# A decoder layer on one core: the order of the work between a residual product and the next product, rewritten

## The chip, the cores and the metric

The kernel runs on one core of a Trainium2 chip. The metric is the device time of one execution in microseconds. The kernel before took 2469.97 us, the median of three runs between 2469.17 and 2472.55.

## The reference

A decoder layer on 256 tokens of 2048 numbers, all in float32. Three sublayers follow, each in the same frame: normalise, modulate by two rows of a conditioning vector, compute, multiply by a gate row, add to x.

```python
mod = (c_act @ w_ada[l] + b_ada[l]).reshape(b, N_MOD, D_MODEL)     # 9 rows of 2048
h = modulate(rms_norm(x, norm_ffn1[l]), mod[:, 0], mod[:, 1])
x = x + 0.5 * mod[:, 2][:, None, :] * swiglu(h, w_ffn1_gu[l], w_ffn1_down[l])
h = modulate(rms_norm(x, norm_mix[l]), mod[:, 3], mod[:, 4])
x = x + mod[:, 5][:, None, :] * token_mixing(h, w_in[l], w_ret_branch[l], w_swa_branch[l],
                                              w_out[l], sinks[l])
h = modulate(rms_norm(x, norm_ffn2[l]), mod[:, 6], mod[:, 7])
x = x + 0.5 * mod[:, 8][:, None, :] * swiglu(h, w_ffn2_gu[l], w_ffn2_down[l])
return rms_norm(x, norm_final)
```

`swiglu` is a product to 2x5632 columns, a gating, and a product back to 2048 (5632 deep). `token_mixing` begins with one wide product `h @ w_in`, from which retention, sliding-window attention and two branch gates take their columns, and ends with the product by `w_out`. The attention's keys are the columns at `O_SK` and its values those at `O_SV`.

## The kernel before

**Tiles.** Tokens are held in two halves t of 128, the depth in blocks kb of 512 (four rows of 128), the columns in chunks of 512. The weights are streamed once. SP's queue loads a block of 512x512 weights as a `raw` tile of 1 MB (`load`, from a pool of four), in the written order.

**Split products.** Every operand of a product is split in two, a rounded part (a cast on ACT) and a remainder (a subtraction on DVE), and each product is the sum of three matmuls: rounded by rounded (L322), remainder of the activation by rounded weight (L323), rounded activation by remainder of the weight (L324). A half block of weights, 128x1024, is cast at L330 (`wh`) and its remainder taken at L331 (`wl`); the pool behind them holds three of each. Splits that have to live longer go to a `home` tile (L402, L403), one of four `slot` buffers. The activations of a residual product are split at L362 and L363 (`a`, or `home`), those of a product behind a normalisation are kept in `Held`, rounded `hh` and remainder `hl`. A half block times both halves of the tokens is 12 matmuls, times one half 6, a whole block times both halves 24.

**The residual product** (`down_product`) stands three times in the program: behind the first SwiGLU, behind the token mixing (by `w_out`), behind the second SwiGLU. It does chunks 0 and 1 first. Of chunks 2 and 3 (`banks[0]` and `banks[1]`) the last three depth blocks, a-1, a and b, are ordered by hand: a loop in which chunk 2 is multiplied, while the weights of chunk 3 are split ahead and kept (`late`), then chunk 3 for t=0 (`last(0, steps)`), then six steps (`tail`) of chunk 3 for t=1, handed to the passage that follows. `add_gated` multiplies a bank by the gate row (L512), adds it to `x_sb` (L513) and has ACT square the result and sum it along the row (L431). `ssq` collects the sums.

**The passage** (`into_norm`, its `before` and `after`) stands behind the first two residual products and runs into the first chunk of the next product (`head`): the `O_SK` chunk of `w_in` the first time, the first gate chunk of the second SwiGLU the second time. `inv_rms` makes the reciprocal root from the sums (L443 to L457). Then the normalised half goes through in four blocks of 512 columns: `normed` scales a block (L477, `x0` to `x3`), `turned` transposes it on PE (L484), `hold` modulates it in four slices, the first ones on ACT (L496), the others on DVE (L498), casts it (L504) and takes the remainder (L505). Two banks hold transposed blocks. A third user of `down_product` is the final normalisation (`final`), which multiplies by the gain row (L1128), scales (L1140, L1144) and sends each chunk out (L1145) through four buffers.

**What sets the order.** A scheduler places the instructions of PE, DVE, ACT and POOL by its own estimate of time; DMAs on SP's queue stay in written order. Within `tc.manual_schedule(engines=ORDERED)` PE, DVE and ACT keep the written order among the instructions of that block, but what is written behind the block may still be placed among them. Such work is the conditioning: `conditioning` loads `w_ada` in rows (L198) and multiplies and sums them on DVE (L203), a step at a time, paced by `set_pace` and `tick` over the half blocks of the products that follow.

**Around the first passage**, POOL's queue copies `x_sb` to memory (`x_d`, L825), since `skt`, the transposed keys, takes the same buffer, loads a few constants (L811, L817, L818) and clears `skt` (L829, L830) and `sv`, the values (L833).

## Time and profile before

| | |
|---|---|
| runs | 2469.17 to 2472.55 us, median 2469.97 of 3 |
| span of the profiled execution | 2465.2 us |
| median less span | 4.8 us, which lie around the span |
| busy: PE | 2410.9 us, 98% of the span, 10910 instructions |
| busy: PE's weight loads | 1981.8 us, 80% |
| busy: DVE | 1701.6 us, 69% |
| busy: ACT | 1195.0 us, 48% |
| busy: POOL | 13.4 us |

The times in the profile are microseconds from the start of the span, of one execution. A line of the timeline gives start, duration, engine, source line, operation, what it writes and from what, and in brackets how long the engine idled before it and for whom. PE's matmuls are pipelined, so the duration of one is longer than the distance between two. The first passage with its residual product's last part lies between 746.79 and 814.20, the second between 1683.11 and 1745.50, the third residual product's last part ends at 2454.45.

### The profile page before, as it was taken

How to read it: one execution, taken by the hardware profiler on the slowest of the kernel's cores; microseconds unless marked ns; L12 is line 12 of the kernel's file. 1: busy time of each engine (PE TensorE's matmuls, PEld its weight loads, DVE VectorE, ACT ScalarE, POOL GpSimd, SP SyncE). 2: the span in 40 equal slices, each digit the busy share in tenths (PEclk: the TensorE clock that was granted, in tenths of full speed). 3: DMA queues.
4: the chain of work that ended last, by engine and by line, in shares of the span. 5: the costliest groups of instructions: out<-in, count | busy, mean ns of one | idle time of the engine just before them, and what ended most of it. 6: DMA issues, size and time to landing. Idle time of an engine off the chain costs nothing. (4 is left out here: it accounts for less than half of the span.)

```text
span 2465.2 us, 29158 instructions
## 1 busy us (share of the span) xinstructions
PE 2410.9 (98%) x10910; PEld 1981.8 (80%) x10910; DVE 1701.6 (69%) x2728; ACT 1195.0 (48%) x1623; POOL 13.4 (1%) x21
## 2 busy tenths in 40 slices
PE   7999999999998999999999999999999999999998
PEld 4778888888786888888888888887788888888886
DVE  6898877777876676786666776767655555545656
ACT  6544544444545554554544444455544444444544
POOL 0000000000000000000000000000000000000000
PEclk9999999999999999999999999999999999999999
DMA  9987687888875665557677777755566666665563
GB/s 355 339 335 268 235 312 297 326 304 303 313 254 206 236 224 205 188 191 253 223 257 255 256 256 257 281 188 179 203 236 227 222 228 232 222 222 191 188 201 120
DMA packets 244656, 603.27 MB, mean 245 GB/s; under 512 B 9697, under 2 KB 10081, under 8 KB 225185
## 3 DMA queue, kind: packets, MB, share of 16 engines
q1 hardware_dynamic: 243010, 591.61, 67.1%
q0 software_dynamic: 1504, 9.81, 1.1%
q8 instruction: 85, 1.39, 0.2%
q14 instruction: 57, 0.47, 0.1%
HBM read 597.16 MB, written 4.22 MB: 244 GB/s over the span
## 5 line engine op out<-in xcount | busy, mean ns | idle before, releaser
L331 DVE TENSOR_TENSOR wl<-raw,wh 128x1024 fp32r<-128x1024 f32 (+1 forms) x828 | 996.6, 1209 | 602.8 <-ACT wh L330 601.3
L330 ACT CAST wh<-raw 128x1024 fp32r<-128x1024 f32 (+1 forms) x828 | 862.6, 1043 | 1044.5 <-PE pa L323 1016.4
L322 PE MATMUL pa<-wh,hh 128*128 128x512 f32 x2224 | 871.9, 393 | 3.8 <-ACT wh L330 2.9
L323 PE MATMUL pa<-wh,hl 128*128 128x512 f32 x2224 | 872.3, 392 | 1.8 <-DVE hl L472 1.8
L324 PE MATMUL pa<-wl,hh 128*128 128x512 f32 x2224 | 805.3, 393 | 3.0 <-DVE wl L331 2.9
L322 PEld LDWEIGHTS pa<-wh,hh 128*128 128x128 f32 x2224 | 418.1, 188 | 93.6 <-ACT wh L330 4.8
L324 PEld LDWEIGHTS pa<-wl,hh 128*128 128x128 f32 x2224 | 416.0, 188 | 92.0 <-DVE wl L331 7.9
L323 PEld LDWEIGHTS pa<-wh,hl 128*128 128x128 f32 x2224 | 418.5, 188 | 87.9 <-DVE hl L472 2.5
L323 PE MATMUL pa<-wh,a 128*128 128x512 f32 x992 | 383.9, 389 | 0.0
L324 PE MATMUL pa<-wl,a 128*128 128x512 f32 x992 | 367.5, 390 | 1.3 <-DVE wl L331 1.2
L322 PE MATMUL pa<-wh,a 128*128 128x512 f32 x992 | 367.2, 390 | 0.3 <-DVE t L512 0.2
L324 PEld LDWEIGHTS pa<-wl,a 128*128 128x128 f32 x992 | 185.7, 188 | 42.2 <-DVE wl L331 4.0
L322 PEld LDWEIGHTS pa<-wh,a 128*128 128x128 f32 x992 | 186.1, 188 | 40.5 <-DVE t L512 0.9
L323 PEld LDWEIGHTS pa<-wh,a 128*128 128x128 f32 x992 | 186.1, 188 | 38.5
L203 DVE CUSTOM_DVE_ANT_0 slot<-slot,cact 128x512 f32<-128x512 f32 (+1 forms) x252 | 193.0, 816 | 27.6 <-DMA slot<-in_w_ada_dram 27.4
L203 DVE CUSTOM_DVE_ANT_0 raw<-raw,cact 128x512 f32<-128x512 f32 (+1 forms) x260 | 167.0, 697 | 36.2 <-DMA raw<-in_w_ada_dram 25.8
L363 DVE TENSOR_TENSOR a<-slot,a 128x512 fp32r<-128x512 f32 x124 | 85.0, 686 | 12.3 <-ACT a L362 12.3
L362 ACT CAST a<-slot 128x512 fp32r<-128x512 f32 x124 | 76.1, 615 | 14.7 <-PE pa L324 14.7
L413 ACT COPY slot<-ps 128x512 f32<-128x512 f32 x75 | 41.7, 586 | 26.3 <-PE ps L412 25.9
L203 DVE DVE_READ_ACCUMULATOR2_ANT sums<- 128x1 f32 x512 | 43.3, 85 | 0.0
L431 ACT ACTIVATE pd<-x_sb 128x512 f32<-128x512 f32 x32 | 19.1, 596 | 42.1 <-DVE x_sb L513 39.4
L412 PE MATMUL ps<-small_c,t 128*128 128x128 f32 x272 | 37.7, 272 | 0.0
(170 smaller groups left out, 1061.6 us busy)
## 6 DMA issues: line engine op xcount, KB each, us to landing
raw<-in_w_ffn_gu_dram SPq DMA_DIRECT2D x152, 1024.0 KB, 5.0
raw<-in_w_in_dram SPq DMA_DIRECT2D x104, 1024.0 KB, 5.0
raw<-in_w_ffn_down_dram SPq DMA_DIRECT2D x88, 1024.0 KB, 5.1
slot<-in_w_ada_dram SPq DMA_DIRECT2D x76, 1024.0 KB, 7.6
raw<-in_w_ada_dram SPq DMA_DIRECT2D x64, 1024.0 KB, 4.8
raw<-in_w_ffn_gu_dram SPq DMA_DIRECT2D x24, 768.0 KB, 6.4
raw<-in_w_swa_branch_dram SPq DMA_DIRECT2D x16, 1024.0 KB, 5.2
raw<-in_w_ret_branch_dram SPq DMA_DIRECT2D x16, 1024.0 KB, 5.3
```

The source lines that it names most:

```text
L203: nc.vector.tensor_tensor_reduce(out=w[:, at], in0=w[:, at], in1=cact[:, at], scale=1.0, scalar=0.0, op0=ALU.mult, op1=ALU.add, accum_out= ...
L322: nc.tensor.matmul(ps, ah[:, j, ts], wh[:, j, :], start=first, stop=False)
L323: nc.tensor.matmul(ps, al[:, j, ts], wh[:, j, :], start=False, stop=False)
L324: nc.tensor.matmul(ps, ah[:, j, ts], wl[:, j, :], start=False, stop=last)
L330: nc.scalar.copy(hi, src)
L331: nc.vector.tensor_sub(lo, src, hi.bitcast(F32))
L362: nc.scalar.copy(hi, v)
L363: nc.vector.tensor_sub(lo, v, hi.bitcast(F32))
L412: nc.tensor.transpose(ps[:, j * P : (j + 1) * P], src_of(j), ident)
L413: nc.any.tensor_copy(dest, ps[:, : n * P])
L431: nc.scalar.activation(side_bank(), src, AF.Square, accum_out=dest)
```

## The change

In `down_product` the loop over the last three blocks splits late weights only in its step a (block a of chunk 3). Those of a-1 and of b are split behind the loop. The products of chunk 3 begin with three half blocks in the order t=0, t=1, t=0, so that `tail` holds five steps of t=1 instead of six. The addition of chunk 2 for t=0 stands ahead of `before`, in which the next product's first weights are split, and the one for t=1 behind it.

In the passage, `hold` becomes `Block`, whose `modulate` (slices and cast) and `rest` (remainder) are called apart, and a half block of weights becomes a `Piece`, whose `cast` and `rest` are called apart. Both halves of weight block 1 are cast ahead of the addition of chunk 3 for t=0. Three blocks of t=0 are scaled before the first transposition, the fourth much later. Weight blocks 2 and 3 are split in pieces between the blocks, partly into `home` tiles. At the end the first weight block of the chunk after the head (`c1`) is split too and handed on as `ready`, and a fence for the scheduler, `tc.no_sync_barrier()`, closes the passage: it keeps what is written behind it from being placed ahead of it, and makes no engine wait.

The conditioning begins eight half blocks later (`idle`). The product of the `O_SV` chunk is written ahead of the transpositions of the keys, and `skt` and `sv` are cleared by DVE behind these, no longer by POOL.

```diff
...
-    def set_pace(outputs, halves, place, ahead):
+    def set_pace(outputs, halves, place, ahead, idle=0):
...
         pace["steps"] = conditioning(outputs, place, ahead)
-        pace["rate"] = len(outputs) * KD * AQ / halves
-        pace["due"] = 0.0
+        pace["rate"] = len(outputs) * KD * AQ / (halves - idle)
+        pace["due"] = -idle * pace["rate"]
...
+    class Piece:
+        def __init__(self, raw, h, home=None, at=0):
+            self.src = raw[:, 2 * h : 2 * h + 2, :]
+            if home is None:
+                self.hi = wsp.tile([P, 2, CH], F32R, tag="wh", name=nm("wh"))
+                self.lo = wsp.tile([P, 2, CH], F32R, tag="wl", name=nm("wl"))
...
+        def cast(self):
+            nc.scalar.copy(self.hi, self.src)
+        def rest(self):
+            nc.vector.tensor_sub(self.lo, self.src, self.hi.bitcast(F32))
...
+    class Block:
...
+            self.h4, self.hi, self.lo = h4, self.held.hi[:, at[0], at[1]], self.held.lo[:, at[0], at[1]]
+            nc.scalar.copy(self.hi, h4)
+            return self
+        def rest(self):
+            nc.vector.tensor_sub(self.lo, self.h4, self.hi.bitcast(F32))
...
             a, b = nb - 2, nb - 1
             home = home_tile().rearrange("p i (h n) -> p (i h) n", h=2)
             pairs, late = {}, {}
+            def late_product(t, kb, h):
+                piece = late[kb, h]
+                products(
+                    banks[1], *pairs[kb][h], piece.hi, piece.lo,
+                    kb + h == 0, kb == b and h == 1, [t],
+                )
+            def late_pieces(kb):
+                raw, place = load(w, kb, c0s[1]), home_tile()
+                for h in range(2):
+                    late[kb, h] = Piece(raw, h, place, h).both()
             for kb in (a - 1, a, b):
-                wt = weight(w, kb, c0s[0])
+                raw = load(w, kb, c0s[0])
                 pairs[kb] = []
                 for h in range(2):
+                    piece = Piece(raw, h).both()
                     place = None
                     if kb >= a:
                         place = home[:, (kb - a) * 2 + h].rearrange("p (i n) -> p i n", i=2)
                     pairs[kb].append(act.pair(kb * 2 + h, place))
                     products(
-                        banks[0], *pairs[kb][h], *wt(h), kb + h == 0, kb == b and h == 1
+                        banks[0], *pairs[kb][h], piece.hi, piece.lo,
+                        kb + h == 0, kb == b and h == 1,
                     )
-                n = kb + 1 if kb < b else a - 1
-                wt = weight(w, n, c0s[1], None if n < a else home_tile())
-                late[n] = [(n, h, wt(h)) for h in range(2)]
-            steps = [step for kb in (a - 1, a, b) for step in late[kb]]
-            def last(t, which):
-                for kb, h, (wh, wl) in which:
-                    products(
-                        banks[1], *pairs[kb][h], wh, wl, kb + h == 0, kb == b and h == 1, [t]
-                    )
-            last(0, steps)
+                if kb == a:
+                    late_pieces(a)
+            raw = load(w, a - 1, c0s[1])
+            for h in range(2):
+                late[a - 1, h] = Piece(raw, h).both()
+            late_product(0, a - 1, 0)
+            late_product(1, a - 1, 0)
+            late_product(0, a - 1, 1)
+            late_pieces(b)
+            for kb in (a, b):
+                for h in range(2):
+                    late_product(0, kb, h)
+            add_gated(banks[0][0], 0, c0s[0], gate, ssq)
+            root_table()
             before()
-            root_table()
-            for t in range(NT):
-                add_gated(banks[0][t], t, c0s[0], gate, ssq)
+            add_gated(banks[0][1], 1, c0s[0], gate, ssq)
             after(
                 ssq,
                 lambda t: add_gated(banks[1][t], t, c0s[1], gate, ssq),
-                [lambda i=i: last(1, steps[i : i + 1]) for i in range(6)],
-            )
-    def into_norm(m_shift, w, c0):
+                [
+                    lambda kb=kb, h=h: late_product(1, kb, h)
+                    for kb, h in ((a - 1, 1), (a, 0), (a, 1), (b, 0), (b, 1))
+                ],
+            )
+    def into_norm(m_shift, w, c0, c1):
         held = Held()
-        nb = KD // KB
         banks = []
-        parts = {}
+        parts, ready = {}, []
         def before():
-            wt = weight(w, 0, c0, home_tile())
+            raw, place = load(w, 0, c0), home_tile()
             for h in range(2):
-                parts[0, h] = wt(h)
+                parts[0, h] = Piece(raw, h, place, h).both()
         def after(ssq, add, tail):
+            def half(t, kb, h):
+                k2 = kb * 2 + h
+                products(
+                    banks, *held.pair(k2), parts[kb, h].hi, parts[kb, h].lo,
+                    k2 == 0, 2 * k2 + 2 == KD, [t],
+                )
             def head(t, kb):
                 for h in range(2):
+                    half(t, kb, h)
+            def block(t, kb, ps, on_act):
+                return Block(held, t, kb, ps, m_shift).modulate(on_act)
+            raw = load(w, 1, c0)
+            for h in range(2):
+                parts[1, h] = Piece(raw, h)
+            parts[1, 0].both()
+            parts[1, 1].cast()
             add(0)
+            parts[1, 1].rest()
+            tail[0]()
+            tail[1]()
             r0 = inv_rms(ssq, 0)
+            raw = load(w, 2, c0)
+            parts[2, 0] = Piece(raw, 0)
+            parts[2, 0].cast()
             x0 = normed(0, r0, 0)
             x1 = normed(0, r0, 1)
             tail[2]()
             tail[3]()
             p0 = turned(x0)
+            x2 = normed(0, r0, 2)
+            b00 = block(0, 0, p0, 2)
+            p1 = turned(x1)
             tail[4]()
+            b01 = block(0, 1, p1, 3)
+            b00.rest()
+            p2 = turned(x2)
+            add(1)
+            b01.rest()
+            banks.extend(acc_bank() for _ in range(NT))
+            head(0, 0)
+            r1 = inv_rms(ssq, 1)
+            b02 = block(0, 2, p2, 4)
+            x0 = normed(1, r1, 0)
+            parts[2, 0].rest()
+            b02.rest()
+            x1 = normed(1, r1, 1)
+            half(0, 1, 0)
+            p0 = turned(x0)
+            half(0, 1, 1)
+            both = home_tile()
+            parts[2, 1] = Piece(raw, 1, both, 0)
+            raw = load(w, 3, c0)
+            parts[3, 0] = Piece(raw, 0, both, 1)
+            parts[2, 1].cast()
+            b10 = block(1, 0, p0, 2)
+            x3 = normed(0, r0, 3)
+            parts[2, 1].rest()
+            b10.rest()
+            parts[3, 0].cast()
+            half(0, 2, 0)
             p1 = turned(x1)
+            half(0, 2, 1)
+            b11 = block(1, 1, p1, 3)
+            parts[3, 0].rest()
+            b11.rest()
+            half(1, 0, 0)
+            p3 = turned(x3)
+            half(1, 0, 1)
+            x2 = normed(1, r1, 2)
+            b03 = block(0, 3, p3, 3)
+            b03.rest()
             p2 = turned(x2)
+            head(1, 1)
+            x3 = normed(1, r1, 3)
+            b12 = block(1, 2, p2, 3)
+            parts[3, 1] = Piece(raw, 1, home_tile(), 0)
+            parts[3, 1].cast()
+            b12.rest()
+            parts[3, 1].rest()
             p3 = turned(x3)
+            head(1, 2)
+            block(1, 3, p3, 3).rest()
+            head(0, 3)
+            head(1, 3)
+            raw = load(w, 0, c1)
+            ready.extend(Piece(raw, h).both() for h in range(2))
+            tc.no_sync_barrier()
+        return held, banks, ready, before, after
...
-    held, head, *calls = into_norm(3, wi, O_SK)
+    held, head, ready, *calls = into_norm(3, wi, O_SK, O_SV)
...
-    set_pace([(7, 2, None), (6, None, None), (5, None, 1.0)], 262, raw_row, 2)
+    set_pace([(7, 2, None), (6, None, None), (5, None, 1.0)], 262, raw_row, 2, 8)
...
-    nc.gpsimd.memset(skt[HD:, 0], 0.0)
-    nc.gpsimd.memset(skt[:HD, 1], 0.0)
     VW = HD + KVH * P
-    sv = slot()[:, : NT * VW].rearrange("p (t n) -> p t n", t=NT)
-    nc.gpsimd.memset(sv, 0.0)
-    b = head
+    b = in_chunk(O_SV, ready)
...
-    b = in_chunk(O_SV)
+    nc.vector.memset(skt[HD:, 0], 0.0)
+    nc.vector.memset(skt[:HD, 1], 0.0)
+    sv = slot()[:, : NT * VW].rearrange("p (t n) -> p t n", t=NT)
+    nc.vector.memset(sv, 0.0)
...
-    held, head, *calls = into_norm(6, w_ffn2_gu[0], 0)
+    held, head, ready, *calls = into_norm(6, w_ffn2_gu[0], 0, DFF)
...
-    set_pace([(8, None, 0.5)], 160, raw_row, 2)
-    ffn_up(held, w_ffn2_gu[0], tiles, 0, head)
+    set_pace([(8, None, 0.5)], 160, raw_row, 2, 8)
+    ffn_up(held, w_ffn2_gu[0], tiles, 0, head, ready)
...
```

With `home` a `Piece` takes its place there. `gemm`, `gemm_part` and `ffn_up` pass `ready` through and use it in place of a first load and split. The old lines of the passage's `after`, which stand in the listing above, are left out of the diff; its lines that carry no sign were there, in another place or the same.

Of the changed kernel's lines, L426 and L429 are the cast and remainder of a `Piece`, L459 the squares, L471 to L485 `inv_rms`, L505 the scaling, L512 the transposition, L530, L534, L541 and L545 the slices, cast and remainder of a `Block`, L552 and L553 the gated addition.

How the orders differ is shown at three places. On ACT, in the loop of the first residual product (`wh` are half blocks of weights used at once, the first `home` is a late weight and takes its two halves, the one from `slot` an activation), before:

```order
L330 CAST wh_5703<-raw_5679 128x1024
L402 CAST home_5719<-raw_5720 128x1024 x2
L362 CAST home_5678<-slot_2511 128x512
L330 CAST wh_5730<-raw_5726 128x1024
L362 CAST home_5678<-slot_2511 128x512
L330 CAST wh_5748<-raw_5726 128x1024
L402 CAST home_5764<-raw_5765 128x1024 x2
L362 CAST home_5678<-slot_2511 128x512
```

and now:

```order
L426 CAST wh_5721<-raw_5719 128x1024
L362 CAST home_5678<-slot_2511 128x512
L426 CAST wh_5739<-raw_5719 128x1024
L362 CAST home_5678<-slot_2511 128x512
L426 CAST home_5759<-raw_5757 128x1024 x2
L426 CAST wh_5766<-raw_5764 128x1024
L362 CAST home_5678<-slot_2511 128x512
L426 CAST wh_5784<-raw_5764 128x1024
```

The late pair ahead of the first activation of block a is gone, and only the one behind block a's step is left.

On ACT, from the addition of chunk 2 to the first transposed block (`pd` takes the squares, `sum` and `rs` are the reciprocal root's), before:

```order
L431 ACTIVATE pd_5872,ssq_4120<-x_sb 128x512
L431 ACTIVATE pd_5879,ssq_4120<-x_sb 128x512
L330 CAST wh_5893<-raw_5874 128x1024
L446 ACTIVATE rs_1039_5899<-sum_5897,eps 128x1
L330 CAST wh_5912<-raw_5874 128x1024
L496 ACTIVATE t_5944<-ps_5928,modc 128x128 x2
```

and now:

```order
L459 ACTIVATE pd_5878,ssq_4120<-x_sb 128x512
L426 CAST wh_5882<-raw_5880 128x1024
L426 CAST wh_5884<-raw_5880 128x1024
L459 ACTIVATE pd_5892,ssq_4120<-x_sb 128x512
L474 ACTIVATE rs_1041_5909<-sum_5907,eps 128x1
L426 CAST wh_5920<-raw_5918 128x1024
L530 ACTIVATE t_5946<-ps_5939,modc 128x128 x2
```

Both casts of weight block 1 now stand ahead of the last squares of t=0, and the root follows the squares at once.

On DVE, from the first slices to the addition of chunk 3 for t=1 (`hl` are remainders of the blocks, `t_5944` and `t_5957` before are blocks 0 and 1 modulated), before:

```order
L498 TENSOR_SCALAR t_5944<-ps_5928,modc 128x128 x2
L505 TENSOR_TENSOR hl_4119<-t_5944,hh_4118 128x4x128
L498 TENSOR_SCALAR t_5957<-ps_5939,modc 128x128
L505 TENSOR_TENSOR hl_4119<-t_5957,hh_4118 128x4x128
L512 TENSOR_TENSOR t_5964<-pa_5035,row_2510 128x512
L203 ISA raw_6268,sums_6267<-raw_6268,cact 128x512
L203 ISA sums_6267 128x1
L203 ISA raw_6268,sums_6267<-raw_6268,cact 128x512
```

(two more such pairs follow ahead of L513), and now:

```order
L505 TENSOR_SCALAR t_5944<-x_sb,rs_1041_5909 128x512
L534 TENSOR_SCALAR t_5946<-ps_5939,modc 128x128 x2
L534 TENSOR_SCALAR t_5963<-ps_5952,modc 128x128
L545 TENSOR_TENSOR hl_4119<-t_5946,hh_4118 128x4x128
L552 TENSOR_TENSOR t_5975<-pa_5035,row_2510 128x512
L553 TENSOR_TENSOR x_sb<-x_sb,t_5975 128x512
L545 TENSOR_TENSOR hl_4119<-t_5963,hh_4118 128x4x128
```

The conditioning is gone from between L512 and L513 (now L552 and L553), the last slice of block 1 stands ahead of block 0's remainder, and block 1's remainder behind the addition.

On POOL, around the first passage, the order was a copy to `x_d`, the clearing of `sv`, the load of `dec`, the other copy, the two clearings of `skt`; now it is the loads of `dec` and of two more constants, and both copies.

115 lines of the change are left out of this document (43 added, 72 removed).

## The prediction

> **What bounds the kernel.** I read the page first, then PE's waits, then the busy time stretch by stretch, then the timeline of the stretches that lose time.
>
> ```profile
> span 2465.2 us, 29158 instructions
> PE 2410.9 (98%) x10910; PEld 1981.8 (80%) x10910; DVE 1701.6 (69%) x2728; ACT 1195.0 (48%) x1623; POOL 13.4 (1%) x21
> PE ps L484 <- DVE t L477: 10.6, 6, 3.3
> ```
>
> PE is the bound, and only 54 us of the span are not PE's. PE's largest wait is a transposition (L484) of a normalised block that DVE has not scaled yet (L477). L484 runs only in the two passages from a residual to the next product. So a change of order there can win only what PE loses there. To size that I need PE's pace when it waits for nothing, from four rows of the timeline:
>
> ```profile
> 759.27 0.39 PE L322 MATMUL pa<-wh,a 128*128 128x512 f32 x1
> ...
> 765.39 0.39 PE L322 MATMUL pa<-home,home 128*128 128x512 f32 x1
> ...
> 1712.13 0.60 PE L484 MATMUL ps<-small_c,t 128*128 128x128 f32 x4
> 1712.48 0.48 PE L322 MATMUL pa<-home,home 128*128 128x512 f32 x1
> ```
>
> Between the first two lie 27 starts, 6.12 us: 0.227 us a matmul. Four transpositions hold the next matmul for 0.35 us, 0.09 each. The stretches (PE's count, less one that still runs from before, is what they had to do):
>
> ```profile
> core 0: us, PE busy (x) PEld busy (x) DVE busy (x) ACT busy (x) POOL busy (x), PEclk, DMA share, GB/s
> 746.79:759.27 12.48, 11.75 (x49) 8.85 (x48) 11.83 (x13) 9.78 (x12) 0.00 (x0) 1.00 1.02 373
> 759.27:773.05 13.78, 13.77 (x61) 11.07 (x59) 7.74 (x14) 5.70 (x12) 0.54 (x1) 1.00 0.67 252
> 773.05:782.10 9.05, 6.59 (x32) 5.21 (x32) 7.05 (x12) 3.47 (x8) 1.91 (x1) 1.00 0.34 116
> 782.10:792.48 10.38, 5.30 (x21) 4.25 (x21) 6.29 (x21) 1.89 (x6) 1.15 (x2) 0.84 0.84 274
> 792.48:814.20 21.72, 19.52 (x88) 15.06 (x89) 13.58 (x18) 15.22 (x28) 3.61 (x2) 1.00 0.32 111
> 1683.11:1695.58 12.47, 11.74 (x49) 8.86 (x48) 11.83 (x13) 9.78 (x12) 0.00 (x0) 1.00 1.01 372
> 1695.58:1721.15 25.57, 23.61 (x109) 18.99 (x108) 16.47 (x35) 10.19 (x22) 0.00 (x0) 1.00 0.38 136
> 1721.15:1745.50 24.35, 19.77 (x91) 14.83 (x90) 15.64 (x28) 16.19 (x31) 0.00 (x0) 1.00 0.18 58
> 2425.45:2454.45 29.00, 28.27 (x121) 22.18 (x119) 22.11 (x34) 12.88 (x20) 0.00 (x0) 1.00 0.27 101
> ```
>
> First passage: 48 matmuls are 10.9 of 12.48 us, lost 1.6; 60 are 13.6 of 13.78, lost 0.2; 24 and 8 transpositions 6.2 of 9.05, lost 2.9; 12 and 8, 3.4 of 10.38, lost 6.9; 72 and 16, 17.8 of 21.72, lost 3.9. Sum **15.5 us**. Second: 48 matmuls, lost 1.6; 96 and 12, 22.9 of 25.57, lost 2.7; 70 and 20, 17.7 of 24.35, lost 6.7. Sum **10.9**. Third residual (no norm product behind it): 120 matmuls are 27.2 of 29.00, less 0.16 of the last one's tail: lost **1.6**. These 28 us are all that the change can reach.
>
> **The change, part by part.** The rows of the first passage that end PE's waits:
>
> ```profile
> 748.40 0.50 PE L324 MATMUL pa<-wl,home 128*128 128x512 f32 x1 [0.64 <-DVE wl L331]
> ...
> 769.78 1.04 ACT L330 CAST wh<-raw 128x1024 fp32r<-128x1024 f32 x1
> ...
> 770.85 1.23 DVE L331 TENSOR_TENSOR wl<-raw,wh 128x1024 fp32r<-128x1024 f32 x1 [1.79 <-ACT wh L330]
> ...
> 771.99 0.15 DVE L443 TENSOR_REDUCE sum<-ssq 128x1 f32<-128x4 f32 x1
> ...
> 773.15 1.91 POOL L833 MEMSET slot<- 128x2176 f32 x1 [3.26 <-PE pa L324]
> 773.34 2.39 DVE L477 TENSOR_SCALAR t<-x_sb,rs 128x512 f32<-128x512 f32 x2
> 775.49 0.63 PE L484 MATMUL ps<-small_c,t 128*128 128x128 f32 x4 [2.45 <-DVE t L477]
> ...
> 781.24 0.68 DVE L512 TENSOR_TENSOR t<-pa,row 128x512 f32<-128x512 f32 x1
> ...
> 781.84 0.68 DVE L203 CUSTOM_DVE_ANT_0 raw<-raw,cact 128x512 f32<-128x512 f32 x1
> ...
> 784.28 0.69 DVE L513 TENSOR_TENSOR x_sb<-x_sb,t 128x512 f32<-128x512 f32 x1
> ...
> 785.42 1.11 PE L484 MATMUL ps<-small_c,t 128*128 128x128 f32 x4 [3.35 <-DVE t L477]
> 786.19 0.78 PE L322 MATMUL pa<-wh,hh 128*128 128x512 f32 x1
> ```
>
> *Late weights out of the product loop.* A step of the loop is 24 matmuls, 5.45 us. DVE's share of it is two weight splits and two of the activations, 2x1.2+2x0.7 = 3.8 us; with two splits of late weights 6.2. That is why PE waits at 748.40. Now only one step carries late splits, with slack ahead of it: 1.6 us won in each of the three loops. The last late pair (2.4 us on DVE) moves behind the loop, under 42 matmuls (9.5 us) in which DVE has about 8.7 us of work; cover gone, it would cost up to 2.4.
>
> *Second split of the first weights cast ahead of the square sum.* The cast at 769.78 stood behind the squares, and DVE with the sum behind its remainder: sum at 771.99. On the new order t=0's bank is full after 42 matmuls, at 757.7+9.5 = 767.2 on this clock (before 767.5), product, addition and square take 0.7+0.7+0.8, so the sum stands at about 770.0. The chain from sum to scaling is 1.35 us, so blocks 0 to 2 are scaled at 771.4 to 772.8. PE has 24 more matmuls, until 772.7: no wait, where 2.45 was.
>
> *Clearings moved from POOL to DVE.* The first L477 ran under the POOL clearing and both took 2.39 us; the second passage has 0.88 (below). Its 1.5 us are part of the 2.45. On DVE, 2176 elements cost 1.9 us at L477's pace (0.44 for 512) and 2.9 at L512's (0.68); I take the dearer, since PE does not see it: it stands behind the passage, under the 24 matmuls whose weights are split ahead, and the pair of 64x2048 (2.7 each at most) stands between two splits where DVE is about 3 us ahead. Cover gone: up to 5 us. The Trainium skill, SBUF — State Buffer, Who interferes with whom, says that a GpSimd instruction and a VectorE one in a two-port mode exclude each other; by that the move wins the same 1.5 us, as the trace has it.
>
> *The fence.* Four conditioning passes (L203) from 781.84 hold up the addition of t=1's bank by 2.4 us, and the transposition at 785.42 behind them. Then PE is slow as well: the stretch from 782.10 was granted 0.84, the first matmul took 0.78. The fence keeps all of it out. It also keeps the next product's matmuls out of PE's gaps; its first block, split ahead, follows at once instead. Starting the conditioning eight halves later changes its rate by 3%: nothing.
>
> *The new order of block 0 and what is late next.* The second passage shows the pass of one block from transposition to remainder without disturbance:
>
> ```profile
> 1709.65 0.88 DVE L477 TENSOR_SCALAR t<-x_sb,rs 128x512 f32<-128x512 f32 x2
> 1710.28 0.63 PE L484 MATMUL ps<-small_c,t 128*128 128x128 f32 x4 [0.94 <-DVE t L477]
> ...
> 1712.61 0.63 ACT L504 CAST hh<-t 128x512 fp32r<-128x512 f32 x1 [0.85 <-DVE t L498]
> 1713.14 1.15 ACT L496 ACTIVATE t<-ps,modc 128x128 f32<-128x128 f32 x3
> 1713.27 0.69 DVE L505 TENSOR_TENSOR hl<-t,hh 128x512 fp32r<-128x512 f32 x1 [0.75 <-ACT hh L504]
> ...
> L498 DVE TENSOR_SCALAR t<-ps,modc 128x128 f32<-128x128 f32 x18 | 7.0, 408 | 9.2 <-ACT t L496 8.9
> ```
>
> 3.0 us from the transposition to the remainder's start, 3.7 to its end, under 12 matmuls and a transposition. The new order has DVE do block 1's last slice before block 0's remainder: it waits for ACT's cast and three slices (1.15). On the first passage's clock: transposition 772.7, cast 775.6, three slices until 776.7, DVE's slice 777.15, remainder 777.85. PE in that time has two groups of transpositions, 6 matmuls and a third group, until 775.5, and then one matmul. It waits **2.4 us**. The rest by the same durations: 17 matmuls to 781.8; the scaling of t=1's block 0 (remainder, addition 1.4, square 0.8, chain 1.35, and 0.6 to PE) lets PE go on at 782.1, **0.3**; the remainder of weights (2,1) stands behind two slices and a scaling on DVE and comes 0.9 after PE needs it, **0.9**; block 2 of t=1 comes **0.45** late; another **0.15** at the third transposition. After that nothing is late and the product ends at 803.1 instead of 814.2. I lose 4.2 in each passage where 15.5 and 10.9 were lost: **11.3 and 6.7 won**. Bounds: without block 0's wait 1.8 stay; if two more blocks come as late as the first, about 7.5.
>
> *The third residual gives its gain back.*
>
> ```profile
> 2446.33 0.69 DVE L512 TENSOR_TENSOR t<-pa,row 128x512 f32<-128x512 f32 x1 [4.29 <-PE pa L324]
> ...
> 2452.99 1.29 DVE L1128 TENSOR_TENSOR t<-x_sb,gf 128x512 f32<-128x512 f32 x2 [1.16 <-DMA out_dram<-t]
> ...
> 2454.06 0.39 PE L324 MATMUL pa<-home,home 128*128 128x512 f32 x1
> 2454.49 0.69 DVE L512 TENSOR_TENSOR t<-pa,row 128x512 f32<-128x512 f32 x1 [0.20 <-PE pa L324]
> ```
>
> PE ends 1.6 us sooner, but t=0's bank is now full six matmuls (1.36 us) nearer to PE's end, since six of t=1 go first. The outputs of t=0, the buffers that DVE waits for at 2452.99 and the two products there (end 2454.28) shift with it; there was 0.2 us between them and L512. So t=1's chain starts 1.2 us later after PE's end: won **0.4**, between -0.2 (a further buffer late) and 1.6 (buffers freed in time).
>
> *Sum.* 11.3+6.7+0.4 = 18.4 us of a span of 2465.2. The median of the runs, 2469.97, is 4.8 above that span; I take what lies around it as unchanged: **2451.6 us**.
>
> **The rivals.** *No new wait* (0.12): ACT and DVE keep ahead and only 1.8 us or less stay lost in each passage. That needs block 0's remainder not to wait for block 1's slice, and the order has it so; 2451.6-2x2.4 = 2446.8, with the third residual's 1.2 kept 2445.6. *DVE takes PE's place* (0.21): in the 36 us from 767 to 803 I count some 26 us of DVE's work in a fixed order; every late row hands its lateness on. Two more blocks as late as the first in each passage: 2451.6+2x3.3 = 2458.2. *A clock that falls in the 2.4 us wait* is the small form of it: six matmuls at 0.43 cost 1.2 us a passage, 2454. The trace has such a fall behind 3.35 idle, none behind 2.45. The Trainium skill, TensorE: Matmul & The Clock Gate, Part 1, puts the fall after an idle window of about 3.4 us; the trace agrees, and by that rule it does not come.
>
> *Slower* (0.02): DVE's clearing of skt waits for both copies of x_sb to memory, and every later weight split stands behind it in DVE's queue.
>
> ```profile
> x_d<-x_sb POOLq DMA_DIRECT2D x2, 1024.0 KB, 7.0
> ```
>
> The clearing's turn comes near 812, its slack is 3 us, and 18.4 us are won; slower than before by 0.2% needs the copies to land after 838. They can be issued from 784 on, and took 7.0. The Trainium skill, SBUF — State Buffer, SBUF: two separate sides, says that VectorE's two-port instructions hold up the descriptors of POOL's DMAs, which the fence has moved into DVE's busiest stretch; no row here shows such a delay. *The change does nothing* (0.03): the fence or the order is undone by other waits, so that the time stays within 0.2%, 5 us, which is about what runs of this kernel can tell.
>
> **How the numbers follow.** My case 0.62, no new wait 0.12, DVE late 0.21, nothing 0.03, slower 0.02. From 2446.5, just under the no-wait case, to 2458.5, the late one, I leave out some 0.15 to 0.2: the outer halves of both and the last two. Faster by over 0.2% is 0.95, the same 0.03, slower 0.02.
>
> **What would show it.** No L203 between the first passage's additions; the scaling at half a microsecond while POOL clears nothing; PE's wait for the transposition of t=0's block 0 gone, one of about 2 us before block 0's second matmul instead; passages of some 56 us (from the loop's second step to the product's end) where 67.4 were; at the end DVE's last product waiting for an output's DMA and not for PE. I am wrong if PE waits at more than three places in a passage, or if the stretch after it, with its clearings, loses time that it did not lose before.

## The result, and the profile after

The changed kernel took 2456.11 us, the median of four runs between 2455.46 and 2457.51, against 2469.57 for the kernel before beside it. The ratio is 0.9946, with a 95% interval from 0.9933 to 0.9958: 13.5 us faster (10 to 17 by the interval). Forecast were 18.4 us less, 2451.6, with a range of 2446.5 to 2458.5. The direction is right, the time lies in the upper half of the range, and 5 us of the expected gain are missing.

One number of the profile before is to be read differently. In every run for which both are on record, the timed execution is 1.7 to 1.8 us longer than its span (2457.51 for the span of 2455.7 below). So the 4.8 us between the median before and the span of 2465.2 do not lie around the span: some 3 of them are scatter, since that profiled execution was a fast one. The one profiled below is the slowest of its four. The two spans therefore differ by 9.5 us only, and the whole is read from the timed runs.

First the head of the page, then PE's waits in the first passage alone (us in total, times, longest).

```profile
span 2455.7 us, 29144 instructions
PE 2410.4 (98%) x10910; PEld 1985.3 (81%) x10910; DVE 1706.5 (69%) x2731; ACT 1192.9 (49%) x1623; POOL 7.7 (0%) x18
...
PE ps L512 <- DVE t L505: 2.3, 1, 2.3
PE pa L323 <- DVE hl L545: 1.6, 1, 1.6
```

PE has the same work as before. In the passage it waits at two places only: for the scaling ahead of the first transposition, and for block 0's remainder. In the second passage it waits at the same two, as long. The busy times by stretch, with the columns that the prediction showed: the two stretches around these waits, then both passages whole.

```profile
772.70:780.26 7.56, 3.67 (x20) 2.48 (x19) 4.55 (x15) 4.58 (x11) 0.00 (x0) 1.00 0.41 139
780.26:784.50 4.24, 4.24 (x12) 3.42 (x13) 3.60 (x11) 2.67 (x9) 2.66 (x5) 0.60 0.47 155
...
746.87:806.14 59.27, 55.38 (x249) 44.82 (x248) 43.18 (x68) 36.57 (x63) 2.66 (x5) 0.97 0.63 224
1677.88:1737.17 59.29, 55.40 (x250) 44.73 (x249) 41.26 (x66) 37.50 (x64) 0.00 (x0) 0.97 0.48 165
```

The first passage took 59.27 us where 67.41 were, the second 59.29 where 62.39 were: 8.1 and 3.1 won, of 11.3 and 6.7 forecast. Behind the two waits the granted clock is 0.60 for 4.24 us. The rest of the time lies closer to before. The last stretch, from the third residual's loop to the end of the span, took 39.28 us (from 2416.42 to 2455.7) instead of 39.75 (from 2425.45 to 2465.2). From the first product to the first passage, where the change hardly reaches, there were 720.4 us before, 721.9 after, and 722.8 in another run of the same changed kernel, so a stretch varies by some us from one execution to the next. Between the passages there were 868.9 before, 871.7 and 869.9 after. That is no mere scatter: the changed kernel has two waits near 1361 us there, which the section on the later start shows.

The rows of the first passage that answer to those of the prediction:

```profile
767.88 0.60 ACT L459 ACTIVATE pd<-x_sb 128x512 f32<-128x512 f32 x1 [2.81 <-DVE x_sb L553]
768.51 1.99 ACT L426 CAST wh<-raw 128x1024 fp32r<-128x1024 f32 x2
769.58 1.23 DVE L429 TENSOR_TENSOR wl<-raw,wh 128x1024 fp32r<-128x1024 f32 x1 [1.74 <-ACT wh L426]
770.72 0.68 DVE L552 TENSOR_TENSOR t<-pa,row 128x512 f32<-128x512 f32 x1
771.44 0.69 DVE L553 TENSOR_TENSOR x_sb<-x_sb,t 128x512 f32<-128x512 f32 x1
772.05 1.22 DVE L429 TENSOR_TENSOR wl<-raw,wh 128x1024 fp32r<-128x1024 f32 x1
773.19 0.15 DVE L471 TENSOR_REDUCE sum<-ssq 128x1 f32<-128x4 f32 x1
774.53 1.28 DVE L505 TENSOR_SCALAR t<-x_sb,rs 128x512 f32<-128x512 f32 x3
775.16 1.07 PE L512 MATMUL ps<-small_c,t 128*128 128x128 f32 x8 [2.29 <-DVE t L505]
...
779.20 0.41 DVE L534 TENSOR_SCALAR t<-ps,modc 128x128 f32<-128x128 f32 x1 [1.80 <-ACT t L530]
779.53 0.68 DVE L545 TENSOR_TENSOR hl<-t,hh 128x512 fp32r<-128x512 f32 x1
780.26 0.80 PE L323 MATMUL pa<-home,hl 128*128 128x512 f32 x1 [1.59 <-DVE hl L545]
...
804.23 1.87 DVE L943 MEMSET slot<- 128x2176 f32 x1 [0.40 <-issue]
826.17 1.76 DVE L940 MEMSET skt<- 64x2048 f32 x1 [0.48 <-issue]
```

The sum stands at 773.19, not at 770.0. The addition of chunk 3 for t=0 (L552) starts at 770.72, because DVE has to take the remainder of weights (1,0) first, which waits 1.74 us for a cast that ACT does behind the squares of chunk 2; the sum then stands behind the remainder of (1,1) as well. Block 0's remainder starts at 779.53, behind block 1's slice, for which DVE waits 1.80 us. The clearings took 1.87 and 1.76 us on DVE. No wait of PE stands behind them.

### The profile page after: what moved, and what is told of

The parts are those of the page before. It is cut to its first block, busy times and chain, and to the rows that moved or that the text cites. A ratio compares the mean times of both kernels' runs of the same rounds, so it can differ in the third digit from the quotient of the medians.

```text
span 2455.7 us, 29144 instructions
## 1 busy us (share of the span) xinstructions
PE 2410.4 (98%) x10910; PEld 1985.3 (81%) x10910; DVE 1706.5 (69%) x2731; ACT 1192.9 (49%) x1623; POOL 7.7 (0%) x18
## 4 chain that ended last, share of the span: by engine, by line
PE 89%; DVE 4%; DMA 1%; ACT 1%; issue 1%; SPq 0%; DVEq 0%; ACTq 0%
PE pa L324 28%; PE pa L323 28%; PE pa L322 28%; PE ps L440 1%; DVE wl L331 1%; DVE slot L203 1%; DMA slot<-in_w_ada_dram 1%; PE pd L962 1%; PE pd L440 0%; DVE home L429 0%; DVE slot L863 0%; PE pd L1024 0%; PE pd L1028 0%; PE pd L1031 0%; PE pd L959 0%
## 5 line engine op out<-in xcount | busy, mean ns | idle before, releaser
L331 DVE TENSOR_TENSOR wl<-raw,wh 128x1024 fp32r<-128x1024 f32 (+1 forms) x788 | 947.6, 1207 | 582.0 <-ACT wh L330 580.2
L330 ACT CAST wh<-raw 128x1024 fp32r<-128x1024 f32 (+1 forms) x788 | 819.5, 1041 | 1043.7 <-PE pa L323 1021.4
L322 PE MATMUL pa<-wh,hh 128*128 128x512 f32 x2200 | 862.4, 393 | 2.2 <-ACT wh L330 1.7
L323 PE MATMUL pa<-wh,hl 128*128 128x512 f32 x2200 | 861.8, 392 | 1.8 <-DVE hl L500 1.8
L324 PE MATMUL pa<-wl,hh 128*128 128x512 f32 x2200 | 796.8, 393 | 2.3 <-DVE wl L331 2.2
L322 PEld LDWEIGHTS pa<-wh,hh 128*128 128x128 f32 x2200 | 413.4, 188 | 89.4 <-ACT wh L330 2.4
L323 PEld LDWEIGHTS pa<-wh,hl 128*128 128x128 f32 x2200 | 413.8, 188 | 87.8 <-DVE hl L500 2.5
L324 PEld LDWEIGHTS pa<-wl,hh 128*128 128x128 f32 x2200 | 410.9, 188 | 89.4 <-DVE wl L331 6.5
L323 PE MATMUL pa<-wh,a 128*128 128x512 f32 x992 | 384.3, 390 | 1.3 <-DVE a L363 1.3
L324 PE MATMUL pa<-wl,a 128*128 128x512 f32 x992 | 368.1, 391 | 1.3 <-DVE wl L331 1.3
L322 PE MATMUL pa<-wh,a 128*128 128x512 f32 x992 | 367.7, 391 | 1.0 <-ACT wh L330 0.5
L324 PEld LDWEIGHTS pa<-wl,a 128*128 128x128 f32 x992 | 185.9, 188 | 42.4 <-DVE wl L331 4.1
L322 PEld LDWEIGHTS pa<-wh,a 128*128 128x128 f32 x992 | 186.6, 188 | 41.4 <-DVE t L552 1.4
L323 PEld LDWEIGHTS pa<-wh,a 128*128 128x128 f32 x992 | 186.5, 188 | 40.3 <-DVE a L363 1.7
L429 DVE TENSOR_TENSOR wl<-raw,wh 128x1024 fp32r<-128x1024 f32 x34 | 41.4, 1223 | 17.4 <-ACT wh L426 17.1
L426 ACT CAST wh<-raw 128x1024 fp32r<-128x1024 f32 x34 | 35.3, 1050 | 17.4 <-PE pa L323 17.3
```

The source lines that it names most:

```text
L322: nc.tensor.matmul(ps, ah[:, j, ts], wh[:, j, :], start=first, stop=False)
L323: nc.tensor.matmul(ps, al[:, j, ts], wh[:, j, :], start=False, stop=False)
L324: nc.tensor.matmul(ps, ah[:, j, ts], wl[:, j, :], start=False, stop=last)
L330: nc.scalar.copy(hi, src)
L331: nc.vector.tensor_sub(lo, src, hi.bitcast(F32))
L426: nc.scalar.copy(self.hi, self.src)
```

## The experiments

All times are medians of four to eleven runs. The runs were made in three groups, and the kernel before took 2470.9, 2469.3 and 2469.0 us beside them: the first holds the changed kernel again and the moves of theory A up to both together, the second the fence alone in either kernel, the conditioning started at once and the loop alone, the third the other four. Between groups the ratios to the kernel before are compared.

### The changed kernel again

> The changed kernel itself, as the measure for the others. Every theory expects 2456 us, between 2455 and 2458, and in each passage the same three losses of PE: 2.3 us before the first transposition, 1.6 us before the second matmul of block 0, and some 8 matmuls at half pace behind it (1.5 us).

It took 2456.7 us (ratio to the kernel before 0.9938, 0.9926 to 0.9950). The first wait, 2.29 us, was as forecast in both passages, which took 58.7 us each. The clock fell sooner, right behind that first wait (0.70 from 777.35 to 783.00), so that block 0's wait shrank to 0.85: the matmuls ahead of it were slow themselves. The sizes of the two later losses depend on where the clock falls.

### Theory A, the first half: what stands ahead of the sum

```diff
-            parts[1, 0].both()
-            parts[1, 1].cast()
             add(0)
-            parts[1, 1].rest()
             tail[0]()
             tail[1]()
             r0 = inv_rms(ssq, 0)
+            parts[1, 0].cast()
+            parts[1, 1].cast()
...
             x2 = normed(0, r0, 2)
+            parts[1, 0].rest()
             b00 = block(0, 0, p0, 2)
             p1 = turned(x1)
             tail[4]()
+            parts[1, 1].rest()
```

> Theory A: PE waits for the first transposition because the addition of chunk 3 for t=0 stands on DVE behind the remainder of weights (1,0) and the sum behind that of (1,1), 1.2 us each, and the squares on ACT behind two casts. With casts and remainders moved behind the scaling the sum stands 2.4 to 3 us sooner, PE's wait of 2.3 us goes in both passages, and the time is 2451 us (2456 - 2x2.4); if the fall of the clock needs both waits, 2448. Rival B: the bank of t=0 is simply full too late, and the chain of addition, square and root is what PE waits for; then the time stays within 1 us of 2456. Rival C: the moved remainders come late for block 1's product and the wait only moves; 2454 to 2456.

2450.7 us, 6.0 less than the changed kernel beside it (ratio to the kernel before 0.9916, 0.9903 to 0.9930). DVE's rows at the place, and the passages:

```profile
768.98 0.68 DVE L552 TENSOR_TENSOR t<-pa,row 128x512 f32<-128x512 f32 x1
769.70 0.69 DVE L553 TENSOR_TENSOR x_sb<-x_sb,t 128x512 f32<-128x512 f32 x1
771.24 0.16 DVE L471 TENSOR_REDUCE sum<-ssq 128x1 f32<-128x4 f32 x1 [0.85 <-ACT pd L459]
772.60 1.28 DVE L505 TENSOR_SCALAR t<-x_sb,rs 128x512 f32<-128x512 f32 x3
...
748.09:803.91 55.82, 53.97 (x249) 43.54 (x248) 43.18 (x68) 36.41 (x63) 2.65 (x5) 1.00 0.69 236
1673.47:1729.27 55.80, 53.95 (x250) 43.53 (x248) 41.26 (x66) 37.35 (x64) 0.00 (x0) 1.00 0.52 174
```

The passage starts 1.22 us later in this execution than in the profile above, so the sum at 771.24 is the 770.0 that was forecast. Of the 3.2 us that it comes sooner, 3.0 lie ahead of the addition, which started at 770.72 and now starts at 767.76 on that clock. That is the remainder of (1,0) and DVE's wait for its cast. The remainder of (1,1) cost only 0.2: the sum has to wait for the squares anyway (1.75 us from the start of L553 to the sum there, 1.54 here). PE's wait for L505 is gone from both passages, and with it the fall of the clock (1.00). So the bank was not full too late (rival B), and the wait did not move (rival C); a new one of 0.3 us, for the remainder of weights (2,1), is the only one beside block 0's 1.6.

### Theory A, the second half: block 0's remainder first

```diff
-            b01 = block(0, 1, p1, 3)
             b00.rest()
+            b01 = block(0, 1, p1, 3)
```

> Only the remainder of block 0 is put ahead of block 1's last slice on DVE. Theory A: PE's wait of 1.6 us before block 0's second matmul is that remainder's, which was ready to start 1.4 us sooner; the wait falls to 0.2 in both passages, 2453 us; and if it is this wait that lets the clock fall, 8 matmuls at half pace go too (1.5 us a passage), 2450. Rival: block 1's cast is late next, since its slice now stands behind the remainder; the time stays within 1 us of 2456.

2454.1 us, 2.6 less than the changed kernel beside it (ratio 0.9925, 0.9912 to 0.9939, which overlaps with the changed kernel's). PE's wait before the second matmul of block 0 is gone from the first passage and 0.2 in the second, and the passages are 0.8 and 1.0 us shorter than the 58.7 beside them:

```profile
746.57:804.52 57.95, 55.23 (x249) 44.84 (x248) 43.27 (x68) 36.43 (x63) 2.65 (x5) 0.97 0.66 227
1676.38:1734.06 57.68, 54.26 (x249) 43.45 (x248) 41.36 (x66) 37.34 (x64) 0.00 (x0) 1.00 0.50 168
```

The clock fell in the first of the two alone. What that shows is below.

### Both moves

The two edits together.

> Both moves. Theory A: PE goes through from the last late product to block 0 without either wait and at full clock; 2x(2.3+1.4+1.5) = 10.4 us less, 2446 us. If the clock falls all the same, 2449. Rival: DVE has no time left in the passage (remainders and slices follow one another from 767 us on), so the two gains do not add up; 2450 to 2453.

2449.2 us (ratio 0.9911, 0.9897 to 0.9924), 7.5 less than the changed kernel, not 10.4. The passages took 55.21 and 55.19 us at full clock, 7.0 us less for the two together; the moves alone had won 5.8 and 1.8 there. So the gains nearly add up in the traces, and the forecast 10.4 was too much: 3.5 us a passage went, not 5.2, since other waits remain. Three show in the first passage:

```profile
PE pa L323 <- DVE hl L545: 0.5, 1, 0.5
PE ps L512 <- DVE t L505: 0.3, 1, 0.3
PE pa L324 <- DVE home L429: 0.2, 1, 0.2
```

The first is what is left of block 0's own wait. The second is the one that the prediction had counted as 0.3, and the third its 0.9, the remainder of weights (2,1). The third stood at 0.23 in the changed kernel's second trace too. In its first trace PE was late enough for DVE to be ahead at both.

To take away the first, the remainder of weights (1,1) was moved once more.

```diff
             tail[4]()
-            parts[1, 1].rest()
             b00.rest()
...
             x0 = normed(1, r1, 0)
+            parts[1, 1].rest()
             parts[2, 0].rest()
```

> Both moves of the earlier run, with the remainder of weights (1,1) put behind the scaling of t=1's block 0 instead of ahead of block 0's remainder. Theory A: what PE still waited for with both moves (0.5 us before block 0's second matmul, 0.3 before the first transposition of t=1, 0.2 for a weight) came from that one remainder of 1.2 us on DVE; the first two go, and each passage takes 54.3 us instead of 55.2: 2447 us. Rival: DVE is full in the passage and hands the lateness on: 2448 to 2451, as with both moves.

2449.5 us (ratio 0.9921, 0.9907 to 0.9934): the same, and the passages took 56.1 us. In the first passage PE's waits became 0.6 (t=1's first transposition), 0.2 and 0.3 for remainders of blocks 0 and 1, and 0.2. The rival is right: a remainder of 1.2 us that leaves one place on DVE makes others late. The two versions with both moves are not told apart by their times. They are the fastest that were found, 0.3% under the changed kernel.

### The fence

```diff
-            tc.no_sync_barrier()
```

> The changed kernel without the fence. The order of DVE then has all three clearings, but none of the conditioning, inside the first passage, ahead of the last slices. The clearings of skt wait for both copies of x_sb to memory, which are issued near 782 us and took 9 us. Theory A: DVE stands there until both have landed and then clears for 5.4 us; PE loses 4 to 6 us: 2460 to 2462. Rival: the order written by hand does all, and DVE has that much slack behind 796 us: 2455 to 2457.

2464.8 us (ratio 0.9982, 0.9972 to 0.9991), 8 to 9 more than the changed kernel. The whole of it is in the first passage, 67.25 us:

```profile
796.59 1.76 DVE L939 MEMSET skt<- 64x2048 f32 x1 [0.49 <-DVE t L505]
798.82 1.76 DVE L940 MEMSET skt<- 64x2048 f32 x1 [0.46 <-issue]
801.13 1.87 DVE L942 MEMSET slot<- 128x2176 f32 x1 [0.40 <-issue]
...
800.00:803.60 3.60, 0.50 (x1) 0.19 (x1) 3.20 (x5) 2.62 (x5) 0.00 (x0) 0.89 0.00 0
803.60:808.00 4.40, 4.39 (x10) 3.47 (x11) 3.46 (x5) 2.96 (x4) 0.00 (x0) 0.50 0.50 146
```

The three clearings stand among block 3's slices. The copies had landed, so DVE did not wait for them; it is the 5.4 us of clearing that PE waits for, 3.7 and 1.7 us, with a clock of 0.50 behind. The loss is larger than forecast by the matmuls that ran slowly behind. The conditioning, from which the prediction took the fence's worth, is not in the passage even without the fence. Whether it is the later start that keeps it out then is open, since no run of the changed kernel leaves out both.

The other way round, the fence alone in the kernel before:

```diff
             head([0, 1], 3)
+            tc.no_sync_barrier()
```

> The kernel before with the fence alone behind its passage. It moves the four conditioning passes from between the additions of t=1 (2.4 us on DVE) and POOL's clearing from under the first scaling (1.5 us). Theory A: PE's waits before the two transpositions fall to what the second passage shows, 0.9 and 1.0 instead of 2.5 and 3.4 us, and no clock falls: 4 to 6 us less than before, 2465 to 2467. Rival: another wait takes their place, such as that for the slices of block 1: 2469 to 2471.

2470.2 us, no change (ratio 1.0004, 0.9995 to 1.0013). Theory A holds for the passage, which took 63.25 us, 4.2 less. But the stretch between the passages took 874.2, 5.2 more. Two places, the first in the passage, the second behind it, where PE waits 2.87 us:

```profile
784.36 2.68 DVE L477 TENSOR_SCALAR t<-x_sb,rs 128x512 f32<-128x512 f32 x2
...
784.43 1.94 POOL L834 MEMSET slot<- 128x2176 f32 x1
...
830.27 2.15 ACT L851 COPY skt<-ps 64x512 f32<-64x512 f32 x4 [5.31 <-PE ps L848]
832.44 2.94 ACT L330 CAST wh<-raw 128x1024 fp32r<-128x1024 f32 x3
```

POOL's clearing of `sv` now meets the scaling of t=1, and ACT stands 5.31 us at copies of the transposed keys with the next weights' casts behind them. What the fence keeps out of the passage collides behind it.

To see whether the keys' place was the cause, the fence was tried with the values' product first and the clearings on DVE behind the keys.

```diff
-    nc.gpsimd.memset(skt[HD:, 0], 0.0)
-    nc.gpsimd.memset(skt[:HD, 1], 0.0)
...
-    nc.gpsimd.memset(sv, 0.0)
-    b = head
+    b = in_chunk(O_SV)
...
-    b = in_chunk(O_SV)
+    nc.vector.memset(skt[HD:, 0], 0.0)
...
+    nc.vector.memset(sv, 0.0)
```

> The kernel before with the fence, the values' product ahead of the keys' transpositions and the clearings on DVE behind them; its own order in the passages, and no weights split ahead. The fence alone won 4.2 us in the first passage and lost 5.2 in the stretch behind it, where PE waited 2.9 us for a cast behind ACT's copies of the transposed keys. Theory A: that loss was the keys' place, and with the values' product ahead of them it goes: first passage 63 us, stretch behind it 869 to 870, 2465 to 2466. Rival: without weights split ahead the first remainder of the next product stands behind the clearing and the keys' copies on DVE, and the loss stays: 2468 to 2470.

2470.3 us (ratio 1.0004, 0.9995 to 1.0013). The first passage took about 62.3 us and the stretch behind it 874.5: the wait of 2.87 us for a cast stayed at the same place, behind the keys' transpositions. The theory falls, and so does the rival's cause, since the first remainder was waited for only 0.75 us. The next run shows the same place with the changed order and the conditioning started at once, and the wait is 1.18 us there; so the later start is part of what spares the changed kernel this wait. Of the rest the traces show how ACT is ordered there: all four copies (2.15 us) ahead of the first cast with the fence in the kernel before, one copy ahead of it with the conditioning at once. Why the scheduler orders them so stays open.

### The later start of the conditioning

```diff
-    set_pace([(7, 2, None), (6, None, None), (5, None, 1.0)], 262, raw_row, 2, 8)
+    set_pace([(7, 2, None), (6, None, None), (5, None, 1.0)], 262, raw_row, 2)
...
-    set_pace([(8, None, 0.5)], 160, raw_row, 2, 8)
+    set_pace([(8, None, 0.5)], 160, raw_row, 2)
```

> The changed kernel with the conditioning started at once, as before, not eight half blocks later. Theory D: the later start moves four passes (L203) to the first blocks of the product by w_swa_branch, between two remainders of its weights, and DVE waits there 2.8 us for a row of w_ada that is still under way; PE loses 1.7 us and then eight matmuls at half pace, near 1361 us in every kernel of this order so far and in none of the kernel before. At once, the passes stand where they stood before, and the time is 3 us less than the changed kernel's, 2453 us. Rival: the row is late for another reason (the weights split ahead shift all loads by one), and the wait stays: 2456.

2455.8 us (ratio 0.9945, 0.9933 to 0.9958), the same as with the later start. The two rows of the changed kernel on which theory D rests, and PE's row of this run that took their place:

```profile
1358.79 0.69 DVE L203 CUSTOM_DVE_ANT_0 raw<-raw,cact 128x512 f32<-128x512 f32 x1 [2.83 <-DMA raw<-in_w_ada_dram]
1363.12 0.50 PE L323 MATMUL pa<-wh,a 128*128 128x512 f32 x1 [1.25 <-DVE a L363]
```

```profile
825.50 0.50 PE L322 MATMUL pa<-wh,hh 128*128 128x512 f32 x1 [1.18 <-ACT wh L330]
```

The wait near 1361 is gone, as the theory said. In its place PE waits 1.18 us at 825, right behind the keys' transpositions, for a cast behind ACT's copies: the place that cost 2.87 with the fence alone. The later start takes one wait away and makes another, and "nothing" is right as a sum. Slow matmuls, which theory D also expected near 1361, stand in two traces only: in the changed kernel's first, and in the run with block 0's remainder first. There the stretch between the passages took 871.7 and 871.9 us. In the changed kernel's second trace the waits are 0.46 and 1.20 with the clock at 1.00 behind them, and the stretch took 869.9, the same as with the conditioning at once.

### The weights split ahead of the fence

```diff
-            raw = load(w, 0, c1)
-            ready.extend(Piece(raw, h).both() for h in range(2))
...
-    b = in_chunk(O_SV, ready)
+    b = in_chunk(O_SV)
```

(and the same in the second SwiGLU.)

> The changed kernel without the next product's first weights split ahead of the fence. The order of DVE then has the clearing of the values (1.9 us) and the four copies of the keys (2.4 us, they wait for the first chunk's end) ahead of the first remainder. Theory A: PE waits some 3 us for that remainder behind the first passage and 0 to 1 behind the second: 2459 to 2460. Rival: the split is done in time anyway, since no engine waits at the fence: 2455 to 2457.

2454.9 us (ratio 0.9945, 0.9933 to 0.9958), against 2456.1 and 2456.7: no difference. PE waited 0.72 us for the first remainder behind the first passage, not 3: DVE made two of the keys' copies at 802.5, while the chunk's other half was still multiplied, and PE had eight transpositions of the keys to do meanwhile. That splitting ahead saves time is not shown.

### The clearings on POOL

```diff
-    nc.vector.memset(skt[HD:, 0], 0.0)
+    nc.gpsimd.memset(skt[HD:, 0], 0.0)
...
-    nc.vector.memset(sv, 0.0)
+    nc.gpsimd.memset(sv, 0.0)
```

> The changed kernel with the three clearings on POOL again, in the new place of the program. POOL's queue has nothing to wait for but buffers and the copies, so it clears inside the passage: 1.9 us near 785 and twice 1.8 near 796. Theory A: a scaling (L505) that falls under a clearing stands until it is over, as in the kernel before (two scalings 2.4 us under 1.9 of clearing instead of 0.9), and PE loses 1 to 3 us in the first passage: 2457 to 2459. Rival: no scaling falls under it, and DVE is 5.4 us freer: 2454 to 2456.

2457.7 us (ratio 0.9954, 0.9942 to 0.9967; 2454.6 to 2461.3), which the measurement does not tell from the changed kernel. That a scaling stands under a clearing is there:

```profile
783.12 2.23 DVE L505 TENSOR_SCALAR t<-x_sb,rs 128x512 f32<-128x512 f32 x1
...
783.13 1.94 POOL L943 MEMSET slot<- 128x2176 f32 x1
```

One scaling takes 2.23 us instead of 0.48 under a clearing of 1.94. But PE is late enough there that no wait follows. The first passage took 59.8 us.

### The loop alone

The kernel before with the late weights split only in the step of block a, those of a-1 and b behind the loop, and the first three half blocks of chunk 3 in the new order, with five steps left for the passage.

```diff
-                n = kb + 1 if kb < b else a - 1
-                wt = weight(w, n, c0s[1], None if n < a else home_tile())
-                late[n] = [(n, h, wt(h)) for h in range(2)]
+                if kb == a:
+                    wt = weight(w, a, c0s[1], home_tile())
+                    late[a] = [(a, h, wt(h)) for h in range(2)]
```

> The kernel before with the new order of the late weights in the loop and of the first three half blocks of chunk 3, nothing else. Theory A: 1.6 us of PE's waits go in each of the three loops, of which the third residual gives 1.2 back: 3.6 us less, 2467. Rival: the late pair behind the loop delays the addition of chunk 2 and with it the sum, and the wait before the first transposition grows by as much: 2469 to 2471.

2466.4 us, 3.0 less (ratio 0.9987, 0.9978 to 0.9996). PE's wait in the loop's second step (0.64 us at 748.40 before) is gone from all three loops. The first passage took 1.7 us less, the last stretch 0.45, and the second passage kept its 62.4, with waits of 0.5 us for block 0's cast (L504) in place of the loop's.

## Why the prediction was right, and where its sizes were off

*Late weights out of the loop*: right. None of the three loops waits, and the loop alone is worth 3.0 us (1 to 5 by the interval); its traces show 1.7 in the first passage, 0.45 at the end and nothing in the second, where other waits took it back.

*Third residual*: right. The last stretch is 0.47 us shorter, where 0.4 was forecast, and ahead of the last addition DVE now waits for an output's DMA, not for PE:

```profile
2445.13 0.69 DVE L552 TENSOR_TENSOR t<-pa,row 128x512 f32<-128x512 f32 x1 [0.15 <-DMA out_dram<-t]
```

*Second split of the first weights cast ahead of the square sum*: this is the step that failed, the sentence "no wait, where 2.45 was". It took the addition of chunk 3 to start when the bank is full. In the written order the remainder of weights (1,0) stands ahead of it on DVE, and the cast that this one waits for stands on ACT behind the squares of chunk 2: 3.0 us of the 3.2 by which the sum was late. The remainder of (1,1), ahead of the sum, made 0.2. With casts and remainders moved the sum came when forecast, the wait went, and the time fell by 6.0 us; the term is 2.3 us a passage plus the slow clock behind it. The second passage of the kernel before, whose wait was 0.94, got a longer one by this order.

*The new order of block 0*: right in place, 1.6 us measured for 2.4 forecast; taken away by one line, it was worth 2.6 us in all by the medians and 1.8 in the passages. The 2.4 is 777.85 less 775.5 and leaves out the one matmul of 0.227 that it names; with it, it is 2.1, and from start to start the trace lost 1.9. Of the 1.8 us of later waits the first trace has none, the second 0.23. When PE came sooner, with both moves, the forecast 0.3 and 0.9 showed as 0.3 and 0.2.

*The second passage's loss*: 10.9 is a little too much. The product there has 72 matmuls in its last stretch, not 70; the trace lacks two records (22 of L324 beside 24 each of L322 and L323). With 216 matmuls and 32 transpositions the passage had 10.5 to lose, and 6.3 to win by the forecast's own account.

*A clock that falls*: forecast as the small form of the second rival, 1.2 us a passage and 2454, and set aside with the Trainium skill, TensorE: Matmul & The Clock Gate, Part 1. It came in both passages of the changed kernel, and near 1364 as well. Eight matmuls ran at up to 0.43 instead of 0.227 us, 1.7 us in the first passage and 1.5 in the second. Waits of 2.3 and 1.6, or 2.3 alone, were ahead of it in the passages, and 0.46 and 1.25 near 1364.

*Clearings and fence*: that the clearings cost nothing on DVE is right where they now stand; without the fence they cost 8 us. The fence was credited with keeping out the conditioning; in the changed order it keeps out the clearings.

*Slower*: nothing waited for the copies of `x_sb`. They took 9.2 us to land instead of 7.0 (6.9 without the fence), and the first clearing of `skt` came at 826.17, more than 30 us after the second had landed. Whether VectorE held them up is not shown: behind the fence both are issued at once, at 782.7 and 783.2, and without it 10 us apart.

*The sign of being wrong*: one of the two came. PE waited at no more than three places in a passage, but the stretch behind the first lost time that it did not lose before, 1.0 us in one trace (869.9 for 868.9) and 2.8 in the other. It was not the clearings, as the forecast feared, but the later start, which it had put at nothing; with the conditioning at once, another wait takes its place.

The sum, then: the forecast lost 4.2 us a passage, the trace shows 7.4 in each (59.27 and 59.29 less 216 matmuls at 0.227 and 32 transpositions at 0.09). From start to start, the first passage's 7.4 are 2.45 at the first wait, 1.9 at block 0's, 1.7 of slow matmuls, and some 1.3 in small pieces, most of them around the transpositions, which the forecast put at nothing. The two passages together lost 6.4 us more than forecast, a little more than the 4.9 that are missing between the timed 13.5 and the forecast. That the time still lies in the range owes something to luck: the wait of block 0 and the later waits, forecast as 2.4 and 1.8, came to 1.9, which made up for part of the wait and the slow clock that were not forecast.

## What to carry to other kernels

When an order is written by hand, walk the queue of each engine that carries the chain, not only the chain: a remainder of 1.2 us, which PE first used 14 us later, held up the addition by 3.0 us with its wait for a cast, because it stood a few lines too high. A part of a change can be worth nothing alone (the fence in the kernel before, 4.2 us won in the passage and 5.2 lost behind it) and be worth 8 us in the company of another. A small wait that is forecast behind a larger one shows only when the larger is gone.

## What the runs showed of the hardware

The granted clock fell behind idle times of 2.3 us, and not always. In the run with block 0's remainder first, the same wait of 2.29 us stands in both passages, and only behind the first did the clock fall:

```profile
774.87:780.50 5.63, 5.63 (x24) 4.84 (x25) 3.39 (x8) 3.10 (x7) 0.06 (x1) 0.70 0.44 166
1704.67:1710.30 5.63, 5.40 (x27) 4.06 (x28) 3.63 (x8) 3.10 (x7) 0.00 (x0) 1.00 0.44 162
```

It fell behind shorter waits too: in the changed kernel behind the 0.46 and 1.25 us near 1361.

```profile
1363.92:1366.70 2.78, 2.78 (x8) 2.21 (x7) 0.88 (x2) 0.03 (x1) 0.00 (x0) 0.51 1.04 396
```

And it stayed at 1.00 behind 0.46 and 1.20 at the same place in the second trace, behind 1.6 in the run with the sum first, and behind 2.45 in the kernel before. So the length of the wait alone does not decide.

The Trainium skill, TensorE: Matmul & The Clock Gate, Part 1, says that the clock falls after an idle window of about 3.4 us, and that the windows run freely. Waits this short should not fill one; the measurement decides. That the phase of such a window is what differs between the two passages would fit, and is not shown.

What a fall costs depends on what waits behind it. The slow matmuls took 1.3 to 1.7 us more in the changed kernel's first trace. But the two passages of the run with block 0's remainder first took 57.95 us with the fall and 57.68 without: there, PE waits 0.8 us for DVE at two places where, behind the fall, it waits 0.15.

A scaling (TENSOR_SCALAR, 128x512) stands still while POOL clears: 2.23 us for one under 1.94 of clearing, 0.48 otherwise. A subtraction (TENSOR_TENSOR) that ran under POOL's clearing of `skt` in the kernel before with the fence kept its 1.22 us.
